# A fused transformer kernel's MLP: weight sums among the activations' sums, splits tied to the norm's scaling, transposes one step ahead, and the last two products row by row

## The chip, the cores and the metric

The kernel is one launch on one core of a Trainium2 chip. The time is the device time of that core in microseconds (us). It has five engines with an instruction queue each: TensorE (PE in the profile, its weight loads are PEld), VectorE (DVE), ScalarE (ACT), GpSimd (POOL) and SyncE (SP), which here only issues DMAs. An engine takes its instructions strictly in the order in which they were built, and waits at one whose semaphores are not there yet. TensorE writes into PSUM, in eight banks of 128 x 512 f32 here.

## The reference

Two transformer blocks on 1024 tokens of width 1024 in f32: first sliding window attention and a pooling mixer, then a block with neighbourhood attention, a gated recurrence and an MLP. The change lies in the MLP and in the last norm, which end the kernel:

```
h = h + mix @ w_o[l]
m = rms_norm(h, norm_mlp[l])
h = h + jnp.square(jax.nn.relu(m @ w_up[l])) @ w_down[l]      # 1024 -> 4096 -> 1024
h = rms_norm(h, norm_final)
return h[:, N_META:]
```

## The kernel before

Every f32 operand of a product is split into a high part (a cast by ScalarE) and a low part (value minus high part, by GpSimd or VectorE). A product then takes three matmuls: high x high, high x low, low x high (mm3, L104). In the MLP both matrix products are done by Strassen's scheme in Winograd's form: seven products of half blocks instead of eight, at the price of sums of blocks before and after. A11, A12, A22 and S1 to S4 name the blocks and sums of the activations.

**Start of the MLP.** While the last output projection runs, last_hook (L1370) stores the rows of X and turns the first half of the tokens (Xa) into xx by transposes. The second half (Xb) is normed by norms(4, 2) and norms(6, 2): squares on ScalarE, twelve Newton steps on small VectorE tiles (newton, L121), then a scaling of each row tile, odd ones on ScalarE (L1326), even ones on VectorE (L1328). first_two(p) (L1459) makes the first two products of column pair p of w_up, A11 and A12, 24 matmuls. For j = 0 to 3 the loop at L1499 makes first_two(j), then sums(j) (L1475): eight transposes of Xb into two banks, then seven VectorE operations (L1482, L119, L1496) and splits on ScalarE and GpSimd that give S1 to S4 and A22 of the second half. w_cols (L86) loads and splits the weights of first_two: cast L79 on ScalarE, subtraction L80 on GpSimd.

**Pairs.** pair(p) (L1529), for p = 0 to 15, makes four weight sums on VectorE (vec, L1515), splits them (split_group, L1506: cast L1510, subtraction L1511), makes the other five products S2, S1, S3, S4, A22 (60 matmuls), adds banks (L1417), takes relu and square (L1455, L1456) and stores seven results to DRAM, four of them (S3, S1, S2, S4) from SyncE's queue. The weight sums of pair p + 1 are ordered behind the first add of pair p.

**Down projection.** Four chunks of 512 rows of w_down, each with seven products of 48 matmuls into four banks (times, L1644). Weights come by load_w11, load_w21 and load_w2 and are combined on VectorE (less, L1623). Activations come back by load_a, X by load_x. into (L1659) adds four banks to X. In the last chunk each row tile is squared and summed (half_done, L1585) and, when both halves of its columns are there, normed, scaled and stored (finish, L1595).

What sets the order: a scheduler places the instructions of each engine by priority (program order) as their inputs get ready, tile pools with a fixed number of buffers make a load or cast wait until an earlier user is done, and `with tc.issue_after(x)` puts the instructions of the block that are on x's engine behind x. It makes no wait on other engines.

Of the kernel before, what the change touches and what calls it, by code (L numbers as in the profile page):

```python
# [19 lines left out]
P = 128  # L20
T = 1024
D = 1024
# [8 lines left out]
def fused_kernel(tc, a, out, stop=None, dbg=None):  # L31
# [1284 lines left out]
    def norms(t0, n):  # L1316
# [121 lines left out]

    blocks = [fa[:, 0:4, :], fa[:, 4:8, :]]

    with ExitStack() as ph:
# [26 lines left out]


# [3 lines left out]
        norms(6, 2)  # L1473

        def sums(j):  # L1475

            pa, pb = turned(xb, j), turned(xb, 4 + j)
# [36 lines left out]
        def vec(out_, x_, y_, op):  # L1514
            nc.vector.tensor_tensor(out=out_, in0=x_, in1=y_, op=op)  # L1515
            return out_

        def raw():
            return wpool.tile([P, 1024], F32, name="wraw", bufs=3).rearrange("p (k c) -> p k c", k=KT)

        def load_raw(p, i):

            if p >= NPR:
                return None
            r_ = wp2.tile([P, KT, P], F32, name="raw") if p else raw()
            nc.sync.dma_start(out=r_, in_=cols(w_up, (2 * p + i) * P)[1])
            return r_

        def pair(p, r1, r2, before_sums=None):  # L1529
            lo_, hi_ = slice(0, 4), slice(4, 8)  # L1530
            tt = raw()
            if p not in open_:
                open_[p] = first_two(p, split_group(r1, KT))
            with tc.issue_after(ready.pop(p)):
                vec(r2[:, lo_], r2[:, lo_], r2[:, hi_], ALU.subtract)
                vec(tt[:, lo_], r1[:, lo_], r2[:, lo_], ALU.subtract)
                vec(tt[:, hi_], r2[:, hi_], tt[:, lo_], ALU.subtract)
                vec(r1[:, hi_], r1[:, hi_], tt[:, lo_], ALU.subtract)
            (b_, u11), c_ = open_.pop(p), bank()
            g = split_group(tt, KT)  # L1540
            product(b_, "S2", [v[:, lo_] for v in g], False)
            u12 = copy_out(b_)
            product(c_, "S1", [v[:, hi_] for v in g], True)
# [3 lines left out]
            product(b_, "S3", [v[:, lo_] for v in g], False)  # L1547
# [3 lines left out]
            product(c_, "S4", [v[:, hi_] for v in g], False)  # L1551
            u12 = activated(add_bank(u12, c_))
            nc.scalar.dma_start(out=d_u["A12"][:, p, :], in_=u12)
            g = split_group(r1[:, hi_], 4)
# [3 lines left out]
            if before_sums:  # L1558
                before_sums()
# [6 lines left out]
        ready = {0: added[0].ins}  # L1566
        rs = {p: [load_raw(p, i) for i in range(2)] for p in range(2)}
# [9 lines left out]
    with ExitStack() as ph:  # L1577
# [7 lines left out]
        def half_done(t, ch):  # L1585

            if t not in fin:
                fin[t] = st.tile([P, 2], F32, name="fin", bufs=NT)
            ss, csl = fin[t], slice(ch * 512, ch * 512 + 512)
            junk = st.tile([P, 1024], BF16, name="junk", bufs=1)  # L1590
            nc.scalar.activation(out=junk[:, csl], in_=X[:, t, csl], func=AF.Square, accum_out=ss[:, ch:ch + 1])
# [3 lines left out]
        def finish(t):  # L1595
            ss, tsl = fin[t], slice(t * P, (t + 1) * P)
            nc.vector.tensor_tensor(out=ss[:, :1], in0=ss[:, :1], in1=ss[:, 1:], op=ALU.add)
            r = rsqrt(ss[:, :1], D)
            if t < NT - 1:
                nc.scalar.activation(out=X[:, t, :], in_=X[:, t, :], func=AF.Copy, scale=r)  # L1600
                nc.sync.dma_start(out=out[tsl, :], in_=X[:, t, :])
            else:
                nc.vector.scalar_tensor_tensor(out=X[:, t, :512], in0=X[:, t, :512], scalar=r, in1=nf[:, :512],
                                               op0=ALU.mult, op1=ALU.mult)
                nc.sync.dma_start(out=out[tsl, :512], in_=X[:, t, :512])
                nc.scalar.activation(out=X[:, t, 512:], in_=X[:, t, 512:], func=AF.Copy, scale=r)
                nc.scalar.dma_start(out=out[tsl, 512:], in_=X[:, t, 512:])
# [3 lines left out]

        def load_w2(c):
            wx = xt.tile([P, KT, 512], F32, name="xh1")
            w12, w22 = [[wx[:, 4 * n + 2 * i:4 * n + 2 * i + 2, :] for i in range(2)] for n in range(2)]
            load_d(w22, 1, 1, c)
            load_d(w12, 0, 1, c)
            return w12, w22
# [119 lines left out]
```

## Time and profile before

| | |
|---|---|
| time, median of 3 runs | 2402.74 us (2401.53 to 2405.03) |
| the profiled execution | 2398.74 us, its span 2396.8 us, mean granted clock of TensorE 0.988 |
| busy share of the span | TensorE 97%, its weight loads 81%, VectorE 59%, ScalarE 40%, GpSimd 32% |
| chain that ended last, by engine | TensorE 84%, VectorE 9%, issue 3%, ScalarE 2%, DMA 1%, GpSimd 1% |
| the MLP in the span | from 1724 to the end |

The runs are timed without the profiler; durations and waits come from the one profiled execution. A start time is in microseconds from the start of the span. In a row, L followed by a number is the line of the kernel, `out<-in` the tiles that an instruction writes and reads, and what stands in brackets is the idle time of the engine before it and what ended it. The granted clock is given as a share of full speed: 1.00 is 2.4 GHz, 0.50 is 1.2 GHz.

### The profile page before, as it was taken

To read this page: it belongs to the slowest core of one execution; us is meant where nothing else is said; L and a number is where in the kernel's file an instruction comes from. 1 tells how busy PE (TensorE), PEld (TensorE's weight loads), DVE (VectorE), ACT (ScalarE), POOL (GpSimd) and SP (SyncE) were. 2 spreads that over 40 slices of the span, in tenths; PEclk is the share of its full clock that TensorE was granted. 3 is DMA by queue.
4 is the path that set the end of the run, shared out by engine and by line. 5 is a ranking of instruction groups with operands and counts; after the bars stand their busy time and mean duration, and the time that the engine had idled before them with its cause. 6 is when DMAs were issued, how large, how long until landed. Compare 5 with 4: busy or idle time off the path is not lost.

```text
span 2396.8 us, 32165 instructions
## 1 busy us (share of the span) xinstructions
PE 2320.8 (97%) x12102; PEld 1932.1 (81%) x12102; DVE 1413.3 (59%) x2647; ACT 960.7 (40%) x1787; POOL 758.8 (32%) x515
## 2 busy tenths in 40 slices
PE   7999999999999999999999999999979999999997
PEld 6877878888877888878888888888757888788885
DVE  5566676644457255553364756866765444777676
ACT  5344452422226354543232323321555555433343
POOL 2112133122225443431211202211434444454454
PEclk9999999999999999999999999999989999999998
DMA  5111114111124221211111111573435444754331
GB/s 159 36 27 36 28 33 109 33 44 58 49 62 150 70 54 49 54 62 44 50 52 54 42 51 49 183 254 117 146 93 188 154 161 159 276 197 163 108 112 71
DMA packets 234011, 230.01 MB, mean 96 GB/s; under 512 B 59832, under 2 KB 174862, under 8 KB 230272
## 3 DMA queue, kind: packets, MB, share of 16 engines
q1 hardware_dynamic: 225040, 210.31, 27.6%
q10 hardware_dynamic: 8224, 16.00, 1.8%
q0 software_dynamic: 592, 1.65, 0.3%
q8 instruction: 95, 1.56, 0.3%
q14 instruction: 60, 0.49, 0.1%
HBM read 168.68 MB, written 59.24 MB: 95 GB/s over the span
## 4 chain that ended last, share of the span: by engine, by line
PE 84%; DVE 9%; issue 3%; ACT 2%; DMA 1%; POOL 1%; SPq 0%; DVEq 0%; ACTq 0%; POOLq 0%
PE mm L111 25%; PE mm L110 25%; PE mm L108 25%; PE A L1129 2%; PE PT L441 1%; PE S L423 1%; PE PT L893 1%; PE S L870 1%; DVE xl L119 1%; DVE r L132 1%; PE tp L1149 1%; DVE s L882 1%; DVE sum L632 1%; DMA d_y<-gate 0%; PE tp L175 0%
## 5 line engine op out<-in xcount | busy, mean ns | idle before, releaser
L108 PE MATMUL mm<-xh,whi 128*128 128x512 f32 (+2 forms) x1744 | 670.5, 385 | 2.9 <-DVE QS L1035 1.5
L110 PE MATMUL mm<-xl,whi 128*128 128x512 f32 (+2 forms) x1744 | 665.4, 382 | 0.0
L111 PE MATMUL mm<-xh,wlo 128*128 128x512 f32 (+2 forms) x1744 | 662.2, 380 | 2.4 <-POOL wlo L80 2.4
L80 POOL TENSOR_TENSOR wlo<-wraw,whi 128x1024 fp32r<-128x1024 f32 (+1 forms) x134 | 319.0, 2386 | 943.8 <-ACT whi L79 892.1
L111 PEld LDWEIGHTS mm<-xh,wlo 128*128 128x128 f32 x1744 | 329.5, 189 | 66.0 <-POOL wlo L80 3.5
L108 PEld LDWEIGHTS mm<-xh,whi 128*128 128x128 f32 x1744 | 329.1, 189 | 63.3 <-DVE QS L1035 1.7
L110 PEld LDWEIGHTS mm<-xl,whi 128*128 128x128 f32 x1744 | 329.4, 189 | 56.1
L79 ACT CAST whi<-wraw 128x1024 fp32r<-128x1024 f32 (+1 forms) x134 | 137.3, 1028 | 387.5 <-PE mm L110 160.5
L111 PE MATMUL mm<-whi,xl 128*128 128x512 f32 (+1 forms) x624 | 222.4, 356 | 0.0
L108 PE MATMUL mm<-whi,xh 128*128 128x512 f32 (+1 forms) x496 | 173.4, 350 | 5.3 <-DVE X L1662 3.9
L110 PE MATMUL mm<-wlo,xh 128*128 128x512 f32 (+1 forms) x496 | 172.8, 348 | 0.6 <-POOL wlo L80 0.6
L111 PEld LDWEIGHTS mm<-whi,xl 128*128 128x128 f32 x624 | 118.5, 190 | 16.7
L108 PE MATMUL mm<-whi,xl 128*128 128x512 f32 x288 | 113.1, 393 | 2.6 <-ACT whi L118 2.2
L110 PE MATMUL mm<-wlo,xl 128*128 128x512 f32 x288 | 113.2, 393 | 2.0 <-POOL wlo L119 2.0
L1511 POOL TENSOR_TENSOR wlo<-raw,whi 128x1024 fp32r<-128x1024 f32 (+1 forms) x42 | 85.6, 2041 | 85.3 <-ACT whi L1510 85.3
L108 PEld LDWEIGHTS mm<-whi,xh 128*128 128x128 f32 x496 | 94.7, 191 | 18.1 <-issue 4.7
L110 PEld LDWEIGHTS mm<-wlo,xh 128*128 128x128 f32 x496 | 94.6, 191 | 12.2 <-POOL wlo L80 0.8
L111 PE MATMUL mm<-whi,ml 128*128 128x512 f32 x256 | 99.6, 392 | 1.6 <-DVE ml L119 1.6
L108 PE MATMUL mm<-whi,mh 128*128 128x512 f32 x256 | 100.2, 391 | 0.1
L110 PE MATMUL mm<-wlo,mh 128*128 128x512 f32 x256 | 99.9, 390 | 0.0
L1515 DVE TENSOR_TENSOR st<-st 128x512 f32<-128x512 f32 x64 | 64.8, 1033 | 54.0 <-ACT st L1456 53.0
L1662 DVE TENSOR_TENSOR X<-X,mm 128x512 f32<-128x512 f32 x112 | 73.0, 682 | 37.9 <-PE mm L111 37.9
(344 smaller groups left out, 4362.1 us busy)
## 6 DMA issues: line engine op xcount, KB each, us to landing
wraw<-in_w_in_dram SPq DMA_DIRECT2D x48, 512.0 KB, 3.9
d_S<-st SPq DMA_DIRECT2D x64, 256.0 KB, 4.6
raw<-in_w_up_dram SPq DMA_DIRECT2D x30, 512.0 KB, 5.3
d_A<-st ACTq DMA_DIRECT2D x48, 256.0 KB, 2.0
fa<-d_S SPq DMA_DIRECT2D x10, 1024.0 KB, 5.1
wraw<-in_pool_w_in_dram SPq DMA_DIRECT2D x18, 512.0 KB, 4.2
fa<-d_A SPq DMA_DIRECT2D x9, 1024.0 KB, 4.9
wraw<-in_attn_w_in_dram SPq DMA_DIRECT2D x32, 256.0 KB, 3.2
```

The costliest lines, as they stand in the source:

```text
L79: nc.scalar.copy(out=hv[:, i:i + n], in_=view[:, i:i + n])
L80: nc.gpsimd.tensor_tensor(out=lv[:, i:i + n], in0=view[:, i:i + n], in1=f(hv[:, i:i + n]), op=ALU.subtract)
L108: nc.tensor.matmul(ps, lhsT=lh[0], rhs=rh[0], start=first and i == 0, stop=False, skip_group_check=chain)
L110: nc.tensor.matmul(ps, lhsT=lh[0], rhs=rh[1], start=False, stop=False, skip_group_check=chain)
L111: nc.tensor.matmul(ps, lhsT=lh[1], rhs=rh[0], start=False, stop=last and i == n - 1, skip_group_check=chain)
L119: (lo_eng or nc.vector).tensor_tensor(out=lo, in0=src, in1=f(hi), op=ALU.subtract)
L132: nc.vector.scalar_tensor_tensor(out=out if i == 2 and out is not None else rv, in0=wv, scalar=-1.5, in1=rv, op0=ALU.add, op1=ALU.mult)
L423: nc.tensor.matmul(sps[j][:, k0:], lhsT=(ql if n == 2 else qh)[rows, qsl], rhs=(kl if n == 1 else kh)[rows, p2, ks], start=n == 0, stop=n ...
L1129: nc.tensor.matmul(aps[:, ch, :], lhsT=kc[:, ch * P:(ch + 1) * P], rhs=pat(Q, ch * P, n, nbc), start=True, stop=True)
L1511: nc.gpsimd.tensor_tensor(out=lv, in0=view, in1=f(hv), op=ALU.subtract)
L1515: nc.vector.tensor_tensor(out=out_, in0=x_, in1=y_, op=op)
L1662: nc.vector.tensor_tensor(out=dst, in0=dst, in1=banks[t], op=ALU.add)
```

## The change

- norms returns its last ScalarE scaling. The weights of first_two(1) to first_two(3) are loaded and split in one block that is ordered on ScalarE behind the scaling of norms(6, 2). The first of them is split in two halves.
- The transposes of step j + 1 are written ahead of first_two and sums of step j.
- The two raw weights of pair 0 are loaded ahead of the loop, and its four weight sums are written behind sums(1). The sums of pairs 1 to 3 are ordered behind those of the pair before, those of later pairs as they were.
- pair collects its four SyncE stores and issues them behind the pair's last load; those of pair 15 come behind load_w2(0).
- In the last chunk the last two products run row tile by row tile (both halves of the contraction for row tile 0, then for 1, and so on). The first four row tiles are finished together, in one set of Newton steps on 128 x 4 values, ordered behind the adds of the product before the last.

```diff
--- before.py
+++ after.py
@@ norms @@
             if j % 2:
-                nc.scalar.activation(out=xn[j], in_=xn[j], func=AF.Copy, scale=r[:, j:j + 1])
+                last = nc.scalar.activation(out=xn[j], in_=xn[j], func=AF.Copy, scale=r[:, j:j + 1])
...
+        return last
@@ load_d: the last load's handle is kept; load_w2 moves up to here unchanged @@
-            nc.sync.dma_start(out=dst[i], in_=wd[:, q:q + 2, j, n * 512:n * 512 + 512])
+            loads[:] = [nc.sync.dma_start(out=dst[i], in_=wd[:, q:q + 2, j, n * 512:n * 512 + 512])]
...
+    loads, stores = [None], []
...
+        def load_raw(p, i):
+
+            if p >= NPR:
+                return None
+            r_ = wp2.tile([P, KT, P], F32, name="raw") if p else raw()
+            loads[:] = [nc.sync.dma_start(out=r_, in_=cols(w_up, (2 * p + i) * P)[1])]
+            return r_
+
+        LO, HI = slice(0, 4), slice(4, 8)
+
+        def weight_sums(r1, r2, tt):
+
+            vec(r2[:, LO], r2[:, LO], r2[:, HI], ALU.subtract)
+            vec(tt[:, LO], r1[:, LO], r2[:, LO], ALU.subtract)
+            vec(tt[:, HI], r2[:, HI], tt[:, LO], ALU.subtract)
+            return vec(r1[:, HI], r1[:, HI], tt[:, LO], ALU.subtract).ins
...
         norms(4, 2)
-        norms(6, 2)
+        with tc.issue_after(norms(6, 2).ins):
+            wf = []
+            for p in range(1, NF):
+                r_ = load_w(cols(w_up, 2 * p * P))
+                wf.append(split_w(r_.rearrange("p (k c) -> p k c", k=KT), [KT, P], cut=2 if p == 1 else 1))
+        r0 = [load_raw(0, i) for i in range(2)] + [raw()]
 
         def sums(j):
 
-            pa, pb = turned(xb, j), turned(xb, 4 + j)
+            pa, pb = banks.pop(j)
...
+        banks = {0: [turned(xb, k) for k in (0, 4)]}
         for j in range(4):
+            if j < 3:
+                banks[j + 1] = [turned(xb, j + 1 + k) for k in (0, 4)]
             if j:
-                open_[j] = first_two(j, w_cols(w_up, 2 * j * P))
+                open_[j] = first_two(j, wf[j - 1])
             sums(j)
+            if j == 1:
+                ready = {1: weight_sums(*r0)}
...
+        def store(order):
+            with tc.issue_after(order):
+                for dst, src in stores:
+                    nc.sync.dma_start(out=dst, in_=src)
+            stores.clear()
+
+        def pair(p, r1, r2, tt=None):
+            if p:
+                tt = raw()
+                if p not in open_:
+                    open_[p] = first_two(p, split_group(r1, KT))
+                with tc.issue_after(ready.pop(p)):
+                    done = weight_sums(r1, r2, tt)
+                if p + 1 < NF:
+                    ready[p + 1] = done
...
             u22 = activated(add_bank(u22, b_))
-            ready[p + 1] = added[0].ins
+            if p + 1 >= NF:
+                ready[p + 1] = added[0].ins
...
-                nc.sync.dma_start(out=d_u[s_][:, p, :], in_=vec(c_, x_, y_, op))
-            nc.sync.dma_start(out=d_u["S4"][:, p, :], in_=vec(u12, u12, c_, ALU.subtract))
+                vec(c_, x_, y_, op)
+                stores.append((d_u[s_][:, p, :], c_))
+            vec(u12, u12, c_, ALU.subtract)
+            stores.append((d_u["S4"][:, p, :], u12))
+            if p < NPR - 1:
+                store(order)
...
-        def finish(t):
-            ss, tsl = fin[t], slice(t * P, (t + 1) * P)
-            nc.vector.tensor_tensor(out=ss[:, :1], in0=ss[:, :1], in1=ss[:, 1:], op=ALU.add)
-            r = rsqrt(ss[:, :1], D)
-            if t < NT - 1:
-                nc.scalar.activation(out=X[:, t, :], in_=X[:, t, :], func=AF.Copy, scale=r)
-                nc.sync.dma_start(out=out[tsl, :], in_=X[:, t, :])
+        def finish(t, n):
+
+            ss = fin[t]
+            nc.vector.tensor_tensor(out=ss[:, :n], in0=ss[:, :n], in1=ss[:, 4:4 + n], op=ALU.add)
+            r = rsqrt(ss[:, :n], D)
+            for i in range(n):
+                tsl = slice((t + i) * P, (t + i + 1) * P)
+                if t < NT - 1:
+                    nc.scalar.activation(out=X[:, t + i, :], in_=X[:, t + i, :], func=AF.Copy, scale=r[:, i:i + 1])
+                    nc.sync.dma_start(out=out[tsl, :], in_=X[:, t + i, :])
...
-        def times(banks, s_, w_, first):
-            for i in range(2):
-                for t in range(4):
...
+        def times(banks, s_, w_, first, by_t=False):
+            for i, t in [(i, t) for t in range(4) for i in range(2)] if by_t else [(i, t) for i in range(2) for t in range(4)]:
...
         w12, w22 = load_w2(0)
+
+        store(loads[0].ins)
         load_x(0, 0)
...
-                nc.vector.tensor_tensor(out=dst, in0=dst, in1=banks[t], op=ALU.add)
+                added[:] = [nc.vector.tensor_tensor(out=dst, in0=dst, in1=banks[t], op=ALU.add)]
                 if done:
                     half_done(4 * h + t, ch)
-                    if ch == 1 - h:
-                        finish(4 * h + t)
+                    if h and not ch:
+                        finish(4 * h + t, 1)
...
-            times(B, *ops, False)
+            times(B, *ops, False, last)
             ops = operands(n + 6, w21)
             into(B, 1, 1, last)
-            times(B, *ops, False)
+            if last:
+                with tc.issue_after(added[0].ins):
+                    finish(0, 4)
+            times(B, *ops, False, last)
```

VectorE in the loop over sums, from the last operation of sums(0) on, in the kernel before. L1496 makes the input of S4, L1417 adds a bank for first_two, L1482 and L119 are operations of sums(1):

```order
L1496 TENSOR_TENSOR st<-fa,st 128x512
L1417 TENSOR_TENSOR st<-st,mm 128x512
L1482 SCALAR_TENSOR_TENSOR st<-mm,vecs,fa 128x512
L1482 SCALAR_TENSOR_TENSOR st<-mm,vecs,st 128x512 x2
L119 TENSOR_TENSOR s2l<-st,s2h 128x512
L119 TENSOR_TENSOR xl_15937<-st,xh_15936 128x512
L1482 SCALAR_TENSOR_TENSOR xl_15937<-mm,vecs,xh_15936 128x512
L1496 TENSOR_TENSOR st<-fa,st 128x512
L1417 TENSOR_TENSOR st<-st,mm 128x512
```

The same place in the changed kernel, where L1533, L1418, L1519 and L119 are these operations, and L1479 are weight sums (wraw: pair 0, raw: pair 1):

```order
L1533 TENSOR_TENSOR st<-fa,st 128x512
L1418 TENSOR_TENSOR st<-st,mm 128x512
L1519 SCALAR_TENSOR_TENSOR st<-mm,vecs,fa 128x512
L1479 TENSOR_TENSOR wraw<-wraw 128x512
L1519 SCALAR_TENSOR_TENSOR st<-mm,vecs,st 128x512 x2
L1479 TENSOR_TENSOR wraw<-wraw 128x512
L119 TENSOR_TENSOR s2l<-st,s2h 128x512
L119 TENSOR_TENSOR xl_15972<-st,xh_15971 128x512
L1519 SCALAR_TENSOR_TENSOR xl_15972<-mm,vecs,xh_15971 128x512
L1533 TENSOR_TENSOR st<-fa,st 128x512
L1479 TENSOR_TENSOR wraw<-wraw 128x512 x2
L1519 SCALAR_TENSOR_TENSOR st<-mm,vecs,fa 128x512
```

Pair 0's sums stand inside sums(1), the first of pair 1 follows ahead of the add of first_two(2), and the order of the sums themselves is kept. On TensorE the transposes of three steps (24, on Xb) now stand in one piece between first_two(0) and first_two(1); before, four stood there, and the next ones among the matmuls of first_two(1).

SyncE's queue where the pairs end and the down projection begins, in the kernel before; wb is w21, xh is the tile of w22 and w12, d_S from st are the last pair's stores, X from d_x are load_x:

```order
L1432 DMA wb<-in_w_down_dram 128x2x512 x2
L1432 DMA xh_18305<-in_w_down_dram 128x2x512 x2
L1562 DMA d_S_14766<-st 128x512
L1562 DMA d_S_14764<-st 128x512
L1562 DMA d_S_14765<-st 128x512
L1563 DMA d_S_14767<-st 128x512
L1432 DMA xh_18305<-in_w_down_dram 128x2x512 x2
L1621 DMA X_18295<-d_x 128x512 x16
```

And in the changed kernel:

```order
L1433 DMA wb<-in_w_down_dram 128x2x512 x2
L1433 DMA xh_18303<-in_w_down_dram 128x2x512 x4
L1559 DMA d_S_14766<-st 128x512
L1559 DMA d_S_14764<-st 128x512
L1559 DMA d_S_14765<-st 128x512
L1559 DMA d_S_14767<-st 128x512
L1654 DMA X_18293<-d_x 128x512 x16
```

The last two transfers of load_w2 have moved ahead of the four stores, and the loads of X follow the stores at once.

## Rows read from the trace of the kernel before

**Rows 1.** What TensorE waited for: engine, line, releaser: us, times, longest

```profile
PE mm L108 <- ACT whi L1510: 12.4, 1, 12.4
...
PE mm L108 <- DVE X L1662: 4.2, 4, 3.7
PE mm L111 <- POOL wlo L1511: 3.7, 4, 1.7
...
PE mm L108 <- ACT whi L118: 2.2, 1, 2.2
PE mm L110 <- POOL wlo L119: 2.0, 1, 2.0
```

**Rows 2.** Busy time by stretch: length, each engine (instructions), clock, DMA share, GB/s

```profile
1900.00:2000.00 100.00, 100.00 (x440) 82.19 (x439) 41.52 (x55) 52.99 (x77) 43.51 (x21) 1.00 0.47 155
1729.70:1789.70 60.00, 40.06 (x166) 31.49 (x165) 39.19 (x52) 31.00 (x50) 24.84 (x15) 0.80 0.31 93
2085.00:2100.00 15.00, 10.82 (x37) 8.19 (x36) 15.00 (x14) 6.10 (x6) 8.38 (x3) 0.77 0.81 300
2366.00:2384.00 18.00, 14.15 (x50) 10.83 (x48) 9.00 (x17) 5.38 (x13) 10.01 (x8) 0.81 0.11 42
```

**Rows 3.** VectorE's timeline: start, us, operation, tiles [idle before, releaser]

```profile
1729.97 0.16 DVE L132 SCALAR_TENSOR_TENSOR r<-w,r 128x2 f32<-128x2 f32 x1
1730.17 2.36 DVE L130 TENSOR_TENSOR w<-r 128x2 f32<-128x2 f32 x1
...
1733.05 1.82 DVE L131 TENSOR_TENSOR w<-w,hx 128x2 f32<-128x2 f32 x1
1734.90 2.27 DVE L132 SCALAR_TENSOR_TENSOR r<-w,r 128x2 f32<-128x2 f32 x1
...
1742.53 0.75 DVE L1482 SCALAR_TENSOR_TENSOR st<-mm,vecs,fa 128x512 f32<-128x512 f32 x1 [3.98 <-PE mm L1335]
...
1767.77 0.74 DVE L1482 SCALAR_TENSOR_TENSOR xl<-mm,vecs,xh 128x512 fp32r<-128x512 f32 x1
```

**Rows 4.** GpSimd's timeline, the splits L80 and L1511

```profile
1730.15 7.00 POOL L80 TENSOR_TENSOR wlo<-wraw,whi 128x1024 fp32r<-128x1024 f32 x3 [0.96 <-ACT whi L79]
...
1771.98 5.91 POOL L1511 TENSOR_TENSOR wlo<-wraw,whi 128x1024 fp32r<-128x1024 f32 x3
```

**Rows 5.** ScalarE's timeline, two casts of the splits

```profile
1728.94 2.08 ACT L79 CAST whi<-wraw 128x1024 fp32r<-128x1024 f32 x2
```

**Rows 6.** VectorE's groups in 1742 to 1771: count, busy us, mean ns

```profile
L1496 DVE TENSOR_TENSOR st<-fa,st 128x512 f32<-128x512 f32 x4 | 5.3, 1328 | 0.0
...
L119 DVE TENSOR_TENSOR xl<-st,xh 128x512 fp32r<-128x512 f32 x4 | 2.7, 686 | 0.2
```

**Rows 7.** TensorE's timeline: pair 0, pair 1, the last matmul

```profile
1771.42 0.79 PE L108 MATMUL mm<-s2h,whi 128*128 128x512 f32 x1 [12.36 <-ACT whi L1510]
...
1789.48 0.39 PE L108 MATMUL mm<-s2h,whi 128*128 128x512 f32 x1
...
2383.45 0.39 PE L111 MATMUL mm<-whi,xh 128*128 128x512 f32 x1
```

**Rows 8.** DMA issues on the page: KB each, median us to landing

```profile
raw<-in_w_up_dram SPq DMA_DIRECT2D x30, 512.0 KB, 5.3
```

**Rows 9.** SyncE's queue: the second half of load_w2

```profile
2075.48 2.00 SPq L1432 DMA_DIRECT2D xh<-in_w_down_dram  x2
```

**Rows 10.** VectorE's timeline, the first less(w12)

```profile
2080.01 1.23 DVE L1625 TENSOR_TENSOR xh<-xh 128x1024 f32<-128x1024 f32 x1 [4.92 <-issue]
```

**Rows 11.** VectorE's timeline at the end: Newton step, four adds, last multiplication

```profile
2366.18 2.27 DVE L132 SCALAR_TENSOR_TENSOR r<-w,r 128x1 f32<-128x1 f32 x1
...
2369.27 2.47 DVE L1662 TENSOR_TENSOR X<-X,mm 128x512 f32<-128x512 f32 x4
...
2390.49 0.75 DVE L1603 SCALAR_TENSOR_TENSOR X<-X,r,nf 128x512 f32<-128x512 f32 x1
```

**Rows 12.** ScalarE's timeline at the end: two scalings

```profile
2361.96 2.19 ACT L1600 ACTIVATE X<-X,r 128x1024 f32<-128x1024 f32 x2 [0.36 <-DVE r L132]
```

More of the change, by code (lines that the diff above doesn't have):

```diff
@@ L1437, in load_w11, with load_w2 @@
                        for _ in range(2)], 0, 0, c)
+    def load_w2(c):
+        wx = xt.tile([P, KT, 512], F32, name="xh1")
+        w12, w22 = [[wx[:, 4 * n + 2 * i:4 * n + 2 * i + 2, :] for i in range(2)] for n in range(2)]
+        load_d(w22, 1, 1, c)
+        load_d(w12, 0, 1, c)
+        return w12, w22
     blocks = [fa[:, 0:4, :], fa[:, 4:8, :]]
+    loads, stores = [None], []
     with ExitStack() as ph:
@@ L1467, in first_two, with vec, raw @@
             return b_, u11
+        def vec(out_, x_, y_, op):
+            return nc.vector.tensor_tensor(out=out_, in0=x_, in1=y_, op=op)
+        def raw():
+            return wpool.tile([P, 1024], F32, name="wraw", bufs=3).rearrange("p (k c) -> p k c", k=KT)
+        def load_raw(p, i):
[10 more added lines that the diff above has]
+            return vec(r1[:, HI], r1[:, HI], tt[:, LO], ALU.subtract).ins
         NF = 4
@@ L1512, in split_group @@
             return hv, lv
[L1514 to L1538, printed above, removed]
+        def store(order):
[12 more added lines that the diff above has]
+                    ready[p + 1] = done
             (b_, u11), c_ = open_.pop(p), bank()
             g = split_group(tt, KT)
-            product(b_, "S2", [v[:, lo_] for v in g], False)
+            product(b_, "S2", [v[:, LO] for v in g], False)
             u12 = copy_out(b_)
-            product(c_, "S1", [v[:, hi_] for v in g], True)
+            product(c_, "S1", [v[:, HI] for v in g], True)
             u22 = copy_out(c_)
@@ L1546, in pair @@
             n2 = load_raw(p + 2, 1)
-            product(b_, "S3", [v[:, lo_] for v in g], False)
+            product(b_, "S3", [v[:, LO] for v in g], False)
             u22 = activated(add_bank(u22, b_))
-            ready[p + 1] = added[0].ins
+            if p + 1 >= NF:
+                ready[p + 1] = added[0].ins
             nc.scalar.dma_start(out=d_u["A22"][:, p, :], in_=u22)
-            product(c_, "S4", [v[:, hi_] for v in g], False)
+            product(c_, "S4", [v[:, HI] for v in g], False)
             u12 = activated(add_bank(u12, c_))
             nc.scalar.dma_start(out=d_u["A12"][:, p, :], in_=u12)
-            g = split_group(r1[:, hi_], 4)
+            g = split_group(r1[:, HI], 4)
             n1 = load_raw(p + 2, 0)
@@ L1557, in pair @@
             u21 = activated(b_)
-            if before_sums:
-                before_sums()
+            order = loads[-1].ins
             for s_, c_, x_, y_, op in (("S3", u11, u21, u11, ALU.subtract), ("S1", u21, u21, u22, ALU.add),
                                        ("S2", stage(), u22, u11, ALU.add)):
-                nc.sync.dma_start(out=d_u[s_][:, p, :], in_=vec(c_, x_, y_, op))
-            nc.sync.dma_start(out=d_u["S4"][:, p, :], in_=vec(u12, u12, c_, ALU.subtract))
+                vec(c_, x_, y_, op)
[4 more added lines that the diff above has]
+                store(order)
             return n1, n2
-        ready = {0: added[0].ins}
-        rs = {p: [load_raw(p, i) for i in range(2)] for p in range(2)}
+        rs = {0: r0, 1: [load_raw(1, i) for i in range(2)]}
         for p in range(NPR - 1):
@@ L1609, in load_w21 @@
         def load_w21(c):
             return load_d([bb.tile([P, 2, 512], F32, name="wb") for _ in range(2)], 1, 0, c)
[L1612 to L1617, printed above, removed]
         def load_x(h, ch):
@@ L1642, in split_b @@
             return res
-        def times(banks, s_, w_, first):
-            for i in range(2):
-                for t in range(4):
-                    tsl = slice(t * P, (t + 1) * P)
-                    mm3(banks[t], [((s_[:, 2 * i + k, tsl], s_[:, 4 + 2 * i + k, tsl]), (w_[i][0][:, k, :], w_[i][1][:, k, :]))
-                                   for k in range(2)], first and i == 0, i == 1, chain=True)
+        def times(banks, s_, w_, first, by_t=False):
+            for i, t in [(i, t) for t in range(4) for i in range(2)] if by_t else [(i, t) for i in range(2) for t in range(4)]:
+                tsl = slice(t * P, (t + 1) * P)
+                mm3(banks[t], [((s_[:, 2 * i + k, tsl], s_[:, 4 + 2 * i + k, tsl]), (w_[i][0][:, k, :], w_[i][1][:, k, :]))
+                               for k in range(2)], first and i == 0, i == 1, chain=True)
         w21 = load_w21(0)
         w12, w22 = load_w2(0)
+        store(loads[0].ins)
         load_x(0, 0)
```

22 lines of the change are left out of this document (12 added, 10 removed).

## The prediction, on record before the changed kernel was run

> **What bounds the kernel now.** I read what TensorE waited for first [rows 1], then a table of stretches [rows 2], then the timelines around the long waits. TensorE is busy nearly the whole span, and where nothing disturbs it 440 matmuls take 100.0 us at a granted clock of 1.00 [rows 2], 0.227 us each. So a change pays only where TensorE stands or runs slowly. In the part that the diff touches there are three such stretches. In 1729.7 to 1789.7 the 132 matmuls of three first_two calls and of pair 0 (30.0 us of work) and 32 short transposes need 60 us. In 2085 to 2100 there are 37 matmuls where 66 would fit, 29 x 0.227 = 6.6 us lost. In 2366 to 2384 there are 50 where 79 would fit, 6.5 us lost. Part of the loss is waiting, the rest is that after each long wait the clock stands at its lower level of 1.2 GHz for some microseconds (the granted clock of the three stretches is 0.80, 0.77 and 0.81). Outside of them the order on the engines is the same but for names, and I cost it at nothing.
>
> **The norm and the three splits.** The last norm's Newton steps are VectorE operations on 128x2 values. One takes 0.16 us, but three of them took 2.36, 1.82 and 2.27 us [rows 3], and each ended with one of GpSimd's three L80 subtractions, which ran without a gap from 1730.15 to 1737.15 [rows 4]. Behind the tie these subtractions start only after the scaling on ScalarE, so the three steps cost 0.5 instead of 6.45 us. The scaling comes some 5.6 us sooner (ScalarE still does relu and square of group 0 first), near 1732.2 instead of 1737.8, where the last of the long steps and three short ones ended. What goes the other way: the casts of the splits (L79, 1.04 us each [rows 5]) now stand between the scaling and ScalarE's first copy in sums(0). That takes ScalarE to about 1736.5, and VectorE's third operation in sums(0) waits for it: 2.0 us lost.
>
> **Transposes ahead.** The 24 transposes of three groups now run in one piece behind first_two(0), and the fourth comes as soon as banks are free. sums(0), which began at 1742.5 [rows 3], can begin near 1733.8: 8.7 us sooner. From there on VectorE is the engine that ends last: once begun, it was hardly idle until 1771, and its groups [rows 6] show the same kind of operation at 0.69 us where it is undisturbed and at 1.33 us where a split of GpSimd stands beside it, 2.6 us over the four steps.
>
> **Weight sums inside.** Pair 0's four sums stood in the last step before, so they move but add nothing to VectorE's total. Four of pair 1 and one of pair 2 now also come before the last operation of sums(3): 5 x 0.6 = 3.0 us (four adds in a row took 2.47 [rows 11]). And GpSimd's work is moved beside the sums: 7.0 us of L80 and 5.9 us of L1511 [rows 4], which lay before and after them. I charge half of these 12.9 us to VectorE, 6.4. So 8.7 - 2.0 - 3.0 - 6.4 = -2.7: the last operation that TensorE wants of the sums, at 1768.5 before [rows 3], ends 2.7 us later, at 1771.2. That is no gain by itself. The gain is what no longer follows: before, the split of pair 0 began only then, TensorE took up work at 1771.4 after 12.4 us, waited 1.7 for GpSimd's half of it [rows 1], and ran at 1.2 GHz at first; pair 1 began at 1789.5 [rows 7]. Now pair 0's weights are split during the sums, and when the sums end, S2 and S1 are all but done. 36 matmuls (S3, S4, A22) are left, 8.2 us. They can start about 0.9 us before the last operation of the sums, whose result only A22 wants: 1771.2 - 0.9 + 8.2 = 1778.5. Gain 11.0. With none of the 12.9 us charged it is 17.4; with all of it 4.6, and the five added operations can each meet a part of a further split, so I take 1 as the low end. Below nothing it can't well go: before, 12.4 us passed with TensorE at rest. The loads of pair 1 wait for the last transpose, then need about 5.3 us each [rows 8]; by my times the two that VectorE wants land 3 us before.
>
> **Pairs 1 and 2.** Their sums are now chained behind pair 0's instead of behind an add of the pair before. The rest of the L1511 wait, 3.7 - 1.7 = 2.0 us [rows 1], lies here, and I take 1.3 of it (0 to 2.0).
>
> **Stores behind the down loads.** The second half of load_w2 was issued at 2075.48, as soon as the last S4 store had its data, and less(w12) started at 2080.01 after 4.92 us for it [rows 9, 10]. That delayed w11's split, for which TensorE waited 2.2 and 2.0 us and then ran at the low clock. Now all four transfers are queued at about 2065, and they have 10 us to land, twice what the first two needed. VectorE can start at 2075.1. Its order changes too: w11 is now second, so its first half is ready near 2077.5, ScalarE and GpSimd have it split by 2081 and the second by 2084.5, while TensorE wants it at 2085.8. I take 6.3 of the 6.6 us. Low end 0: the X loads, behind the stores in both kernels, or the added transfers could hold VectorE as long. Below nothing no row points, since the stores' data come at the same time and are wanted two chunks later.
>
> **Last two products.** TensorE's wait of up to 3.7 us for L1662 [rows 1] is a bank that the adds had not emptied: VectorE was held in a Newton step of 2.27 us beside a GpSimd split [rows 11]. Row by row, bank 0 is emptied while the next three rows run, and the steps of rows 0 to 3 come after the adds. What is late next: the second half of the last weights can't be cast before a buffer is free, which is now at 7/8 of the product before, near 2365.2, instead of 1/2; with cast and split it is there at about 2369.1, and TensorE wants it at 2368.1. So 1.0 of the 6.5 us stays and TensorE ends near 2378.3 instead of 2383.8 [rows 7]. Behind it stand four scalings of 1.1 us each on ScalarE [rows 12], moved there by the batch: they fill 2372.3 to 2376.6, the squares of rows 4 to 6 come after them, and the last multiplication ends near 2386.2 instead of 2391.24 [rows 11]. The stores behind it then take the same 5.6 us to the end of the span. Gain 5.0. High end 9.0: in the kernel before, four rows' steps stand behind the last matmul, now perhaps one. Low end -1, if the scalings and splits meet worse than I laid them.
>
> **Sum.** 11.0 + 1.3 + 6.3 + 5.0 = 23.6 us; with all low ends 0, with all high ends 35. Against the profiled execution of 2398.74 (1.94 over its span) that is 2375.1; the median of the runs stands 4.0 higher, so I forecast 2402.74 - 23.6 = 2379.1.
>
> **Rivals.** (1) GpSimd eats the start. All 12.9 us and the five added operations are charged: the first term is 1 to 4 instead of 11, the time 2388. For it: each of rows 3's three steps lost nearly a whole GpSimd instruction, though it needed 0.16. Against it: inside the sums before, one operation in seven lost 0.64 us. The Trainium skill ("SBUF — State Buffer", section "SBUF: two separate sides") says that a VectorE operation with two SBUF inputs and a GpSimd operation exclude each other for a whole instruction; by it the stall is moved from the norm into the sums, where three of seven operations have two SBUF inputs. The trace agrees so far as rows 3 and 4 go.
> (2) GpSimd hardly disturbs: 17.4 and more at the start, 2372.
> (3) The store tie does nothing, because less(w12) then waits for loads that share the bandwidth: without the 6.3 us 2385.4.
> (4) Slower: the low clock. The work is now cut into pieces with short waits for banks and splits between; if TensorE stays at 1.2 GHz there, the 132 matmuls at the start take 2 x 30 us, and with the transposes pair 0 ends some 7 us later than before instead of 11 sooner, and the 96 matmuls at the end take 96 x 0.2 = 19 us more, less the 6.5 lost already: 7 + 13 - 6.3 - 1.3, about 12 us slower, 2415. It decides from a granted clock of about 0.6 over both stretches. Against it: the low clock followed waits of 3.7 us and more, and the 0.80 of rows 2 is mostly one wait of 12.4.
>
> **How the numbers follow.** Forecast 0.63 (own range 2373 to 2386), rival 1 0.16, rival 2 0.11, rival 3 0.06, rival 4 0.04. For 8 in 10 I go from 2370 to 2391, which takes in rivals 1 to 3 at their centres. A change of 0.2% (4.8 us) is what can be told from none: within it only a start and an end that both fail, 0.02, taken from rival 1; faster 0.94, slower 0.04.
>
> **What will show it.** Norm: no Newton step over 0.3 us before the scaling, Xb scaled near 1732. Start: no TensorE wait for the split of pair 0, the last sums near 1771, pair 1 near 1778.5; if VectorE's two-input operations there average over 1.5 us, rival 1 holds. Junction: no wait for L118's and L119's splits of w11, clock 1.00 in the 15 us. End: one wait of about 1 us for the last split, TensorE done some 12 us after the product before, and the span 13 us after that. I am wrong if sums(0) does not begin 8 us sooner, or if the waits come back as waits for banks at a low clock.

## The result and the profile after

The changed kernel takes 2380.62 us (median of 4 runs, 2379.78 to 2381.95) against 2402.14 (2400.16 to 2405.03) in the same comparison: ratio 0.991, 95% interval 0.9893 to 0.9927, so faster by 21.5 us. The forecast was 2379.1, a gain of 23.6.

The profiled execution took 2379.78 us with a span of 2378.0, 18.8 under the span of before. I cut both traces at the same events: T0, the first Newton step of the last norm (L141 on `nm`); T1, the first S2 matmul of pair 1; T2, the matmul behind the last pair's 0.34 us wait for an add (2061.22 before, 2052.72 after); T3 and T4, the matmuls behind the 0.18 us waits of the first and the last chunk (2136.79 and 2289.97; 2122.61 and 2275.83); then the end of the span.

| stretch | before, us | after, us | gain | forecast |
|---|---|---|---|---|
| T0 to T1, start of the MLP | 60.31 | 50.67 | 9.64 | 11.0 |
| T1 to T2, pairs | 271.74 | 270.70 | 1.04 | 1.3 |
| T2 to T3, junction | 75.57 | 69.89 | 5.68 | 6.3 |
| T3 to T4, chunks | 153.18 | 153.22 | 0.0 | 0 |
| T4 to the end, tail | 106.83 | 102.17 | 4.66 | 5.0 |
| sum | 667.63 | 646.65 | 20.98 | 23.6 |

The 2.18 us missing from the span's gain lie ahead of T0 (1729.17 before, 1731.35 after), where nothing was changed. In the 14 traces of this study T0 lies anywhere from 1728.74 to 1734.62, while one kernel's stretches repeat closely: in the four experiments that leave the start as it is, T0 to T1 is 50.2 to 50.8. So the stretches, each from one trace, are compared below; the times of whole runs tell only larger differences (in the comparisons of the experiments, the kernel before had medians from 2400.33 to 2403.28).

The changed kernel by stretch, with the three of [rows 2] moved to the same work (length, each engine's busy time, granted clock, DMA share, GB/s):

```profile
1731.88:1791.88 60.00, 50.61 (x209) 38.84 (x208) 50.12 (x61) 35.15 (x57) 34.77 (x19) 0.91 0.40 123
2076.50:2091.50 15.00, 15.00 (x68) 12.43 (x67) 15.00 (x13) 6.88 (x7) 11.34 (x4) 1.00 0.55 201
2351.86:2369.86 18.00, 11.57 (x50) 8.94 (x48) 13.28 (x44) 9.65 (x16) 7.97 (x6) 0.95 0.30 121
```

The first stretch holds 209 matmul records where it held 166, at a clock of 0.91 instead of 0.80; the second is full at 1.00; in the third the same 50 are done in 11.57 us of busy time instead of 14.15. What TensorE waited for from 1717 on, which answers to [rows 1]:

```profile
PE mm L108 <- DVE st L1418: 2.5, 3, 1.5
PE mm L108 <- DVE xl L1519: 2.5, 1, 2.5
PE mm L1336 <- DVE xl L1519: 2.3, 1, 2.3
PE mm L1336 <- DVE Xb L1328: 1.5, 1, 1.5
PE mm L108 <- ACT whi L118: 1.1, 1, 1.1
PE mm L110 <- POOL wlo L119: 1.0, 1, 1.0
```

The wait of 12.4 for pair 0's split is gone, and no single wait is over 2.5 us. VectorE's timeline at the start, which answers to [rows 3]: scaling, first operation of sums(0), two subtractions beside L80, last operation of the sums, pair 2's weight sums, the adds:

```profile
1734.00 0.75 DVE L1328 TENSOR_SCALAR Xb<-Xb,r 128x1024 f32<-128x1024 f32 x1
1735.90 0.75 DVE L1519 SCALAR_TENSOR_TENSOR st<-mm,vecs,fa 128x512 f32<-128x512 f32 x1 [1.15 <-PE mm L1336]
...
1740.06 1.47 DVE L119 TENSOR_TENSOR s2l<-st,s2h 128x512 fp32r<-128x512 f32 x1 [0.28 <-ACT s2h L118]
1741.45 2.86 DVE L119 TENSOR_TENSOR xl<-st,xh 128x512 fp32r<-128x512 f32 x1
...
1772.94 0.74 DVE L1519 SCALAR_TENSOR_TENSOR xl<-mm,vecs,xh 128x512 fp32r<-128x512 f32 x1
1773.60 1.51 DVE L1479 TENSOR_TENSOR wraw<-raw 128x512 f32<-128x512 f32 x1
1775.15 2.77 DVE L1479 TENSOR_TENSOR wraw<-raw,wraw 128x512 f32<-128x512 f32 x1
1777.84 0.68 DVE L1479 TENSOR_TENSOR raw<-raw,wraw 128x512 f32<-128x512 f32 x1
1778.44 1.27 DVE L1418 TENSOR_TENSOR st<-st,mm 128x512 f32<-128x512 f32 x2
```

TensorE at the marks that [rows 7] has for before: S3 of pair 0, A22 of pair 0, S2 of pair 1, the last matmul:

```profile
1772.73 0.50 PE L108 MATMUL mm<-s3h,whi 128*128 128x512 f32 x1
...
1779.17 0.50 PE L108 MATMUL mm<-xh,whi 128*128 128x512 f32 x1 [0.70 <-DVE st L1418]
...
1782.02 0.39 PE L108 MATMUL mm<-s2h,whi 128*128 128x512 f32 x1
...
2364.05 0.39 PE L111 MATMUL mm<-whi,xh 128*128 128x512 f32 x1
```

### The profile page after: what moved, and what is told of

It reads as the page before. It is cut to its first block, busy times and chain, and to the rows that moved or that the text cites. A ratio compares the mean times of both kernels' runs of the same rounds, so it can differ in the third digit from the quotient of the medians.

```text
span 2378.0 us, 32146 instructions
## 1 busy us (share of the span) xinstructions
PE 2317.6 (97%) x12102; PEld 1929.5 (81%) x12102; DVE 1409.7 (59%) x2623; ACT 961.9 (40%) x1788; POOL 762.4 (32%) x516
## 5 line engine op out<-in xcount | busy, mean ns | idle before, releaser
L80 POOL TENSOR_TENSOR wlo<-wraw,whi 128x1024 fp32r<-128x1024 f32 (+1 forms) x135 | 319.8, 2374 | 949.1 <-ACT whi L79 910.4
L1479 DVE TENSOR_TENSOR st<-st 128x512 f32<-128x512 f32 x64 | 63.2, 1008 | 58.0 <-ACT st L1465 56.9
```

What stands on the lines that cost most here:

```text
L80: nc.gpsimd.tensor_tensor(out=lv[:, i:i + n], in0=view[:, i:i + n], in1=f(hv[:, i:i + n]), op=ALU.subtract)
L1479: return nc.vector.tensor_tensor(out=out_, in0=x_, in1=y_, op=op)
```

## The experiments

E1 to E10 start from the changed kernel, with one thing undone or altered (E10 two); E11 and E12 combine what paid. Measured, in us: T0 to the first operation of sums(0) and to the end of the last operation of the sums, then the stretches; the time is the median of 4 runs (5 for E12):

| | sums begin | sums end | start | pairs | junction | tail | time |
|---|---|---|---|---|---|---|---|
| before | 13.36 | 39.34 | 60.31 | 271.74 | 75.57 | 106.83 | 2402.14 |
| changed | 4.55 | 42.33 | 50.67 | 270.70 | 69.89 | 102.17 | 2380.62 |
| E1 stores back | 4.54 | 41.81 | 50.20 | 270.75 | 75.27 | 102.14 | 2387.44 |
| E2 tail back | 4.54 | 41.82 | 50.16 | 270.80 | 69.91 | 105.82 | 2384.61 |
| E3 rows only | 4.53 | 42.31 | 50.65 | 270.87 | 69.89 | 106.73 | 2385.18 |
| E4 batch only | 4.54 | 42.42 | 50.80 | 270.87 | 69.91 | 101.13 | 2378.35 |
| E5 untied | 9.27 | 43.44 | 52.07 | 270.80 | 69.86 | 102.13 | 2379.79 |
| E6 transposes back | 4.53 | 39.47 | 47.61 | 270.75 | 69.89 | 102.19 | 2376.82 |
| E7 sums late | 4.53 | 34.10 | 57.23 | 271.80 | 69.90 | 101.83 | 2386.74 |
| E8 no low parts | 4.54 | 39.08 | 47.56 | 270.90 | 69.86 | 102.16 | 2375.38 |
| E9 pair sums later | 4.54 | 39.13 | 47.35 | 271.72 | 69.91 | 101.88 | 2376.52 |
| E10 sums inside only | 9.07 | 40.48 | 50.29 | 273.68 | 69.90 | 102.10 | 2384.01 |
| E11 E6 with E4 | 4.53 | 39.48 | 47.87 | 270.38 | 70.20 | 101.18 | 2375.38 |
| E12 E11, pair 1 tied | 4.54 | 39.72 | 49.16 | 273.71 | 69.88 | 101.16 | 2380.11 |

**E1, stores back.**

```diff
                 vec(c_, x_, y_, op)
-                stores.append((d_u[s_][:, p, :], c_))
+                nc.sync.dma_start(out=d_u[s_][:, p, :], in_=c_)
...
-        store(loads[0].ins)
```

> The changed kernel with the stores of each pair issued again as soon as their data are there, the last pair's ahead of the second half of load_w2. Stretch that decides: from the 0.34 us wait of the last pair to the 0.18 us wait of the first chunk, 75.57 us before (2061.22 to 2136.79) and 69.89 after (2052.72 to 2122.61). Theory (the four parts pay each for itself, and this one pays because w12 lands early): the stretch goes back to 75.6, the waits for L118's and L119's splits of w11 come back, the rest stays; time 2386.3. Rival (less(w12) is late anyway, the loads share the bandwidth; then the stretch became shorter by something else, VectorE's order): at most +1, 2381.5.

The junction went back to 75.27. SyncE issued the second half of load_w2 at 2069.83, behind the last store, and VectorE and TensorE waited as in [rows 1, 10]. VectorE's first less(w12) in E1, then TensorE's waits there:

```profile
2074.41 1.23 DVE L1656 TENSOR_TENSOR xh<-xh 128x1024 f32<-128x1024 f32 x1 [4.97 <-issue]
```

```profile
PE mm L108 <- ACT whi L118: 2.2, 1, 2.2
PE mm L110 <- POOL wlo L119: 1.7, 1, 1.7
```

So the store tie alone is worth 5.4 us here; the rival falls.

**E2 to E4, the tail.** E2 undoes both parts, E3 keeps the products row by row, E4 keeps the batch.

In E2 and E4, at both of the last two products:

```diff
-            times(B, *ops, False, last)
+            times(B, *ops, False)
```

In E2 and E3:

```diff
-                    if h and not ch:
+                    if ch == 1 - h:
                         finish(4 * h + t, 1)
...
-                with tc.issue_after(added[0].ins):
-                    finish(0, 4)
```

> The changed kernel with the last two products again half by half of the contraction and each row finished by itself. Stretch that decides: from the 0.18 us wait of the last chunk to the end of the span, 106.83 us before (2289.97 to 2396.8), 102.17 after (2275.83 to 2378.0). Theory: back to 106.8, with a wait of some 3.7 us for the add of bank 0; time 2385.3. Rival (the last 100 us are set by the stores and the scalings, whatever the order of the products): within 1 us of 102.2.

> The changed kernel, last two products row by row, but each of rows 0 to 3 finished by itself again. Theory (the wait for bank 0 goes because the bank is done a quarter through the product and has 8 us to be emptied, so the Newton steps may stand where they like): no wait for an add over 0.5 us, the wait of 1.0 for the last split stays, the stretch to the end 103.2, one over the changed kernel for steps beside GpSimd; time 2381.6. Rival (the batch of Newton steps is what frees VectorE, the order of the products does little): 106 to 107, 2385.

> The changed kernel with the finish of four rows in one batch behind the adds, but the products half by half. Theory: the Newton steps no longer stand ahead of the adds, so the wait for bank 0 falls from 3.7 to under 1 us, and the weight buffer is free at half of the product, so the wait of 1.0 for the last split goes; TensorE ends within 1 us of the changed kernel, but rows 4 to 7 become ready within the last 3/8 of the product instead of a quarter each, so the span ends 1 to 2 us later: stretch 103.7, time 2382.1. Rival (row by row is what counts): the wait stays over 3 us, 106 to 107, 2385.

E2 gives the wait of 3.69 for bank 0 back (tail 105.82). That is 1.0 under before, although the instructions and the waits of the tail are the same. TensorE's clock differs: from 1.1 us ahead of the end of that wait on, before and then in E2 (the granted clock is third from the end):

```profile
2369.00:2377.60 8.60, 7.50 (x22) 6.00 (x23) 2.71 (x6) 3.93 (x9) 5.02 (x4) 0.61 0.15 62
```

```profile
2355.10:2363.70 8.60, 7.49 (x26) 6.07 (x27) 2.72 (x6) 3.93 (x9) 5.02 (x4) 0.80 0.16 62
```

So the two edits account for 3.65 of the 4.66 (105.82 to 102.17), and the other 1.0 goes with how long the clock stayed low in the one trace of before. Which of the two is usual no run shows.

E3 has no wait for a bank, as expected, and yet gains nothing: 106.73, as its rival had it. TensorE's waits in E3, then ScalarE where they arise:

```profile
PE mm L108 <- ACT whi L118: 4.4, 1, 4.4
PE mm L110 <- POOL wlo L119: 1.9, 1, 1.9
```

```profile
2356.26 1.15 ACT L1640 ACTIVATE X<-X,r 128x1024 f32<-128x1024 f32 x1 [1.90 <-DVE r L132]
...
2357.93 1.03 ACT L118 CAST whi<-wb 128x1024 fp32r<-128x1024 f32 x1
```

The cast of the last half of the weights is queued on ScalarE behind a scaling that waits for row 3's Newton steps. In the changed kernel it ran ahead of the batch's scalings:

```profile
2351.27 1.06 ACT L118 CAST whi<-wb 128x1024 fp32r<-128x1024 f32 x1 [0.18 <-issue]
...
2358.14 4.29 ACT L1640 ACTIVATE X<-X,r 128x1024 f32<-128x1024 f32 x4 [4.33 <-DVE r L132]
```

E4, the batch without the row order, has no wait over 0.4 us behind T4 and a tail of 101.13, a microsecond under the changed kernel, where 1.5 over it was expected; E11 and E12, which have the same tail, repeat it (101.18 and 101.16). The batch brings the whole gain; the row order costs 1.0, and the changed kernel's wait of 1.00 for the last split, whose buffer comes free later, is not there in E4.

**E5, untied.**

```diff
-        with tc.issue_after(norms(6, 2).ins):
-            wf = []
+        norms(6, 2)
+        if True:
+            wf = []
```

> The changed kernel without the tie of the three splits to the norm's scaling. Stretch that decides, here and in the next three: from the first Newton step of the last norm to the first S2 matmul of pair 1, 60.31 us before (1729.17 to 1789.48), 50.67 after (1731.35 to 1782.02). Theory (the stretch is bound by VectorE, and the tie moves GpSimd's work from the norm into the sums): the scaling comes 4 to 6 us later, but sums(0) gets back the 3.0 us that two of its operations lost beside L80 and 1.5 us of waiting for ScalarE, so the stretch is 52.2, time 2382.1. Rival (the tie is worth the whole of what the norm lost, 5.6 us): 56.3, 2386.2.

Start 52.07: the theory's number (the time, 2379.79, is not 1.4 over the changed kernel's, but whole runs do not tell differences as small as this). In E5 VectorE's Newton steps are held again beside L80:

```profile
1729.35 1.26 DVE L131 TENSOR_TENSOR w<-w,hx 128x2 f32<-128x2 f32 x1
1730.64 1.19 DVE L132 SCALAR_TENSOR_TENSOR r<-w,r 128x2 f32<-128x2 f32 x1
1731.86 2.26 DVE L130 TENSOR_TENSOR w<-r 128x2 f32<-128x2 f32 x1
```

The sums begin 4.7 us later than in the changed kernel and end 1.1 later: most of what the tie takes from the norm it puts into the sums.

**E6, transposes back.**

```diff
-            pa, pb = banks.pop(j)
+            pa, pb = turned(xb, j), turned(xb, 4 + j)
...
-        banks = {0: [turned(xb, k) for k in (0, 4)]}
...
-            if j < 3:
-                banks[j + 1] = [turned(xb, j + 1 + k) for k in (0, 4)]
```

> The changed kernel with the transposes of step j written again in step j. Theory (VectorE is the bound, and the first eight transposes still come at once): sums(0) begins at the same time, later steps wait little, the stretch is 51.7, time 2381.6. Rival (the transposes ahead are what lets VectorE run without a gap): each of the steps 1 to 3 waits for its transposes behind the 24 matmuls of first_two, some 2 us each, 56 to 57, 2386.5.

Both were wrong: without the transposes ahead the start is 3.1 us shorter, 47.61. The sums begin at the same time and end 2.9 sooner. The loads of pairs 1 and 2 take Xb's memory, so they are issued when the last transpose is done: SyncE's queue in the changed kernel, then in E6:

```profile
1747.72 4.95 SPq L1489 DMA_DIRECT2D raw<-in_w_up_dram  x4
```

```profile
1757.04 4.92 SPq L1489 DMA_DIRECT2D raw<-in_w_up_dram  x4
```

With the loads early, the order placed four weight sums of pair 1 and one of pair 2 ahead of the last operation of the sums; in E6 only two stand there. E9 tests whether that is the cost.

**E7, sums late.**

```diff
-            if j == 1:
-                ready = {1: weight_sums(*r0)}
...
+        with tc.issue_after(added[0].ins):
+            weight_sums(*r0)
...
-            if p + 1 >= NF:
-                ready[p + 1] = added[0].ins
+            ready[p + 1] = added[0].ins
```

> The changed kernel with the four weight sums of pair 0 written behind the loop, behind the add of first_two(3), and the sums of pairs 1 to 3 again behind the first add of the pair before. Theory: seven weight sums and GpSimd's splits leave the sums, which VectorE ends some 10 us sooner than in the changed kernel; then TensorE waits some 8 to 12 us for pair 0's split as before. Net: stretch 54, pairs 1 and 2 wait again for their splits (1 us), time 2385. Rival (the wait of 12.4 us comes back in full and nothing is won in the sums): 61, 2391. Second rival (the weight sums inside bring nothing, the earlier norm brought it all): 50.7, 2380.6.

57.23 lies between theory and first rival, and the pairs cost 1.1 more, as expected. VectorE ended the sums 8.2 us sooner than in the changed kernel, and TensorE then waited in E7 for pair 0's split:

```profile
1771.06 0.79 PE L108 MATMUL mm<-s2h,whi 128*128 128x512 f32 x1 [7.57 <-ACT whi L1550]
...
1773.54 0.80 PE L111 MATMUL mm<-s2h,wlo 128*128 128x512 f32 x1 [1.27 <-POOL wlo L1551]
```

**E8, no low parts.**

```diff
-                wf.append(split_w(r_.rearrange("p (k c) -> p k c", k=KT), [KT, P], cut=2 if p == 1 else 1))
+                hv = wpool.tile([P, 1024], F32R, name="whi").rearrange("p (k c) -> p k c", k=KT)
...
+                wf.append((hv, wu0[1]))
```

> The changed kernel without the low parts of the weights of first_two(1) to first_two(3): their four L80 subtractions on GpSimd (7.70 us) are left out and the low part of first_two(0)'s weights is used in their place, with as many matmuls. It prices GpSimd's work beside VectorE. Theory (the prediction's charge of a half): the two operations of sums(0) that took 1.47 and 2.86 us fall to 0.7 each, the stretch is 3.0 to 3.9 us shorter, 47.2, time 2377. Rival 1 (all of it is charged): 7.7 us shorter, 43.0, 2373. Rival 2 (hardly disturbs): within 0.7 of 50.7.

The sums end 3.25 us sooner and the start is 3.1 shorter, 42% of the 7.70 us taken from GpSimd. VectorE's two operations in E8:

```profile
1738.72 1.37 DVE L119 TENSOR_TENSOR s2l<-st,s2h 128x512 fp32r<-128x512 f32 x1 [0.28 <-ACT s2h L118]
1740.01 0.68 DVE L119 TENSOR_TENSOR xl<-st,xh 128x512 fp32r<-128x512 f32 x1
```

The second fell from 2.86 to 0.68; the first kept most of its length, now beside another GpSimd split, L119's of S3.

**E9, pair sums later.** s4 is the operation of sums(3) that makes S4's input.

```diff
-                ready = {1: weight_sums(*r0)}
+                weight_sums(*r0)
+        ready = {1: s4}
...
-            if p + 1 >= NF:
-                ready[p + 1] = added[0].ins
+            ready[p + 1] = added[0].ins
```

> The changed kernel, transposes ahead kept, with the weight sums of pair 1 ordered behind the last operation of sums(3) that makes the input of S4, and those of pairs 2 and 3 behind the first add of the pair before; pair 0's stay inside sums(1). It tells why the kernel of e6 was 3.1 us faster than the changed one. Theory A (the transposes ahead made VectorE's order take four weight sums of pair 1 among the activations' sums; the sums themselves are the cost): the start is 47 to 48, as in e6, the last operation of the sums ends near +38.5 instead of +42.3, and pairs 1 and 2 cost up to 1 us more. Theory B (the transposes themselves cost, by banks held or by TensorE's order): the start stays 50 to 51.

Theory A: start 47.35 with all transposes ahead, sums ending 3.2 sooner, pairs 1.0 dearer. So the cost behind E6 is the weight sums among the activations' sums.

**E10, sums inside only.** E5's and E6's edits together.

> Of the three edits at the start only the weight sums inside are left: no tie to the scaling, transposes in their own step; stores and tail as in the changed kernel. Theory (the sums inside are the whole gain at the start, tie and transposes ahead give and take): the start is 47.6 + 1.4 = 49.0, against 50.7 in the changed kernel and 60.3 before; time 2379.0. Rival (without the tie the sums start as late as before, +13.4 instead of +4.5, and the gain is only what the weight sums save at the end of it): 55 or more, 2385.

Neither. The start is 50.29, 10.0 under before. E10 differs from E6 by the tie alone, and its start is 2.7 longer; with the transposes ahead the tie was worth 1.4 (E5). The first operation of sums(0) in E10, which waited 3.98 before [rows 3]:

```profile
1739.26 0.75 DVE L1520 SCALAR_TENSOR_TENSOR st<-mm,vecs,fa 128x512 f32<-128x512 f32 x1 [1.42 <-PE mm L1336]
```

Another 3.0 us are lost in the pairs, where VectorE stood at a weight sum of pair 3 whose load had not landed, with an add queued behind it that TensorE wanted. It came back in E12, whose rows stand below.

**E11 and E12, combinations.** E11 is E6 with E4; E12 is E11 with `ready = {1: s4}` as in E9, and the chain from pair 1 to 3 kept.

> The changed kernel with the transposes in their own step (as e6) and the last two products half by half with the batched finish (as e4). If the two gains are independent: start 47.6, tail 101.1, together 4.1 us under the changed kernel, 2376.0 (its median 2380.6 in the first comparison). Rival (the gain of 1.0 at the tail was the scatter of one execution): tail 102.2, 2377.2.

> The kernel of e11 with the weight sums of pair 1 ordered behind the input of S4 of sums(3), the sums of pairs 2 and 3 chained behind them as in the changed kernel. Expected if the weight sums among the last activations' sums are still the cost: two of the three that stand before the last operation of the sums leave (2 x 0.6 us), the start is 46.6 against 47.6 to 47.9 in e6 and e11, pairs 270.7, tail 101.2, 1.2 us under e11: 2374.2. Rival (pair 1's split, now later, makes TensorE wait at pair 1, or TensorE's 36 last matmuls are the bound): no gain, 2375.4 or more.

E11 took 2375.38 us (2374.50 to 2376.04), ratio to before 0.9893 (0.9876 to 0.9909). From T0 on it is 3.8 us shorter than the changed kernel (642.85 against 646.65), and its slowest run is under that kernel's fastest; the intervals of the ratios overlap. E12 was to gain 1.2 and lost 4.7, of which 3.3 lie in the pairs. VectorE, then TensorE, there:

```profile
1786.37 0.69 DVE L1479 TENSOR_TENSOR raw<-raw 128x512 f32<-128x512 f32 x1 [7.13 <-DMA raw<-in_w_up_dram]
```

```profile
1794.26 0.50 PE L108 MATMUL mm<-xh,whi 128*128 128x512 f32 x1 [2.88 <-DVE st L1418]
```

The chain brought pair 3's first weight sum to VectorE ahead of the add. In E11 the same operation waited 1.24 us for its load. The other 1.3 lie in the start: ahead of pair 1, TensorE waited 0.97 for an operation of the sums and 0.99 for an add that stood behind a weight sum of pair 2 of 2.86 us; E11 has neither wait.

## Why the prediction was right

The four places and the direction held, and each size within 1.4 us. Three of the reasons did not hold: that the transposes ahead bring sums(0) forward and cost nothing, that the row order brings the gain at the tail, and that the clock falls only behind waits of 3.7 us and more (last section).

- **The norm.** Forecast: the scaling 5.6 us sooner. Measured from T0: 2.65 instead of 8.62, 6.0 sooner. The size is right; the tie brings 4.2 of it. Without the tie (E5, E10) the scaling starts 6.9 after T0, where the L80 splits ahead of it took 4.8 instead of 7.00 [rows 4].
- **Transposes ahead.** Forecast: sums(0) 8.7 sooner. Measured 8.8 (4.55 against 13.36), but E6 has the same 4.53 without them. What E5 and E10 lack is the tie, and there the sums begin at 9.1 to 9.3. The rest, 4.1 to 4.3 us, came from neither: 1.7 to 1.8 of it is that earlier scaling, and 2.3 to 2.6 a shorter wait of sums(0) for its transposes, 1.66 in E5 and 1.42 in E10 instead of 3.98. Before, seven matmuls are recorded between the transposes that start at 1738.60 and those at 1742.08, in E10 one. Which edit moved them no run took apart. Transposes ahead were costed at nothing but cost 3.1, through the loads that they let start and the weight sums that came with these.
- **Weight sums inside.** Five added operations were put at 3.0 us; taking pairs 1's and 2's away (E9) ended the sums 3.2 sooner. The mechanism is right: without pair 0's inside (E7) the wait for its split is back, 6.6 us in the start.
- **GpSimd beside VectorE, half charged.** E8: 42% for L80; the other part of the charge, L1511, no run left out by itself. Rivals 1 and 2 (all, or hardly anything) fall. Among operations with two SBUF inputs the stall takes whole pieces (0.68 against 2.86), and L1519, which reads one operand from PSUM, was never held: 16 of them in the sums at a mean of 0.74, while the four s2l average 1.70 (line, operation, count, busy us, mean ns):

```profile
L119 DVE TENSOR_TENSOR s2l<-st,s2h 128x512 fp32r<-128x512 f32 x4 | 6.8, 1696 | 0.3 <-ACT s2h L118 0.3
L1519 DVE SCALAR_TENSOR_TENSOR st<-mm,vecs,st 128x512 f32<-128x512 f32 x8 | 5.7, 741 | 1.6 <-ACT st L1522 1.5
```

By the Trainium skill ("SBUF — State Buffer", section "SBUF: two separate sides") only VectorE operations with two SBUF inputs, or in a mode that takes both ports, exclude GpSimd; these rows agree. How much of GpSimd's time is charged then depends on which operations stand beside it.
- **The size of the start.** The sums were to end 42.0 after T0 (1771.2) and ended at 42.33. Pair 1 was to begin at 49.3 and began at 50.67. The term that was short is the last 36 matmuls: 8.2 us forecast, 9.29 measured (1772.73 to 1782.02), with a wait for L1418 in it. That add stood on VectorE behind pair 2's weight sums, which the prediction counted but did not follow past the sums. Undone one at a time, the weight sums inside are worth 6.6, the tie 1.4 and the transposes ahead -3.1, together 4.9; the other 4.7 of the start's 9.64 no single run shows.
- **Pairs.** 1.04 of 1.3, but not as forecast. Before, TensorE waited three times for L1511 (0.67, 0.68 and 0.61). These waits are gone, and a new one of 1.49 for L1418 came at 1794.55, where the chain put pair 3's weight sums ahead of the add; the prediction had it at nothing. E7 and E9, without the chain, have the three waits again and not the new one. That the size came near is in part luck.
- **Junction.** Right, and E1 shows it by itself. It came out 0.6 short, with a wait of 1.14 for a cast at 2100.43, not forecast.
- **Tail.** The forecast wait of 1.0 for the last split measured 1.00; TensorE gained 5.26 from T4 to its last matmul (93.48 to 88.22), 5.5 forecast. The step "bank 0 is emptied while the next three rows run" names the wrong edit: E3 does that and gains nothing, E4 does not and gains all. The batch takes the Newton steps from before the adds and the scalings from before a cast. The last multiplication came 3.9 us sooner, 5.0 forecast, and the stores behind it took 4.8 instead of 5.6, where the same was forecast. With the 1.0 of the clock (E2), the nearness of 4.66 to 5.0 is in part luck.
- **Rivals 3 and 4** fall with E1 and with the clocks of the three stretches (0.91, 1.00, 0.95).

## What to carry to other kernels

An edit that lets a transfer start sooner also moves what waits for it; look in the new order at what lands among work that bounds the stretch. A chain of ties on an in-order engine is priced by the transfer that its last link waits for and by what is queued behind it. When two edits share a gain, run each without the other before crediting either.

## What the runs showed of the hardware

I had expected the low clock only behind waits of 3.7 us and more, against my own rows: at the junction the clock was 0.77 [rows 2] behind waits of 2.2 and 2.0 [rows 1]. In the changed kernel it followed shorter ones: waits of 2.32, 0.90 and 0.85 between 1742.8 and 1748.5, and one of 2.48 before 1767.1; behind one of 1.48 before 1734.8 it stayed full. The changed kernel by stretch, the granted clock third from the end:

```profile
1736.00:1742.00 6.00, 5.46 (x26) 4.18 (x25) 4.09 (x5) 5.60 (x9) 5.94 (x4) 1.00 0.32 88
1748.50:1753.20 4.70, 4.66 (x11) 3.70 (x12) 4.70 (x8) 2.34 (x4) 1.28 (x1) 0.50 0.82 247
...
1767.10:1770.50 3.40, 3.38 (x8) 2.69 (x9) 3.40 (x5) 3.40 (x7) 3.38 (x3) 0.52 0.00 0
```

So a wait of 2.5 us cost about 1.6 us more in the 8 matmuls behind it (3.4 us at 0.52, against 8 x 0.227 = 1.8 at the full clock, [rows 2]). It does not do so each time: E1 and E2 have this wait too (2.49 and 2.48), and there the clock stayed full. E2, from 0.2 us ahead of the end of the wait on:

```profile
1767.00:1770.50 3.50, 2.98 (x11) 1.89 (x11) 3.50 (x6) 3.50 (x8) 3.48 (x3) 1.00 0.00 0
```

The starts of E1 and E2 are about 0.5 us shorter than those of the changed kernel, E3 and E4.
